# A decoder trunk on one core: the feed-forward output products in fp16 pairs, with scales found on the chip

## The chip, the core and the metric

The kernel runs on one NeuronCore of one Trainium2 chip. TensorE (PE in the profile) multiplies matrices from SBUF into PSUM banks of 128 rows by 512 columns, VectorE (DVE) and ScalarE (ACT) do the elementwise work, GpSimd (POOL) a little of it, and SyncE (SP) issues the transfers between device memory and SBUF. Each engine works through its own instructions in order and waits for the others by semaphores. The metric is the time of one execution on the device in microseconds (us), the median of several.

## What is computed

A trunk of two layers on 1024 tokens of width 1024, batch 1, in float32. Layer 0 mixes tokens with a gated linear recurrence (RG-LRU), layer 1 with stick-breaking attention; each is followed by a feed-forward part with 2816 hidden columns:

```python
def swiglu_ffn(x, w_in, w_out):
    gu = jnp.einsum("bsd,df->bsf", x, w_in)
    h = jax.nn.silu(gu[..., :D_FF]) * gu[..., D_FF:]
    return jnp.einsum("bsf,fd->bsd", h, w_out)

for layer in range(DEPTH):
    hn = rms_norm(h, mix_norm[layer])
    h = h + mixer(hn)
    h = h + swiglu_ffn(rms_norm(h, ffn_norm[layer]), ffn_w_in[layer], ffn_w_out[layer])
return rms_norm(h, final_norm)
```

## The kernel before

**Split operands.** To come near float32 on TensorE each operand is written as a high and a low part, and each block product takes three matmuls: high by high, high by low, low by high (`mm3`, lines 155 to 157). Two kinds of pairs occur. An *fp32r pair* takes two 4-byte tiles: ScalarE casts (CAST), VectorE subtracts (TENSOR_TENSOR). An *fp16 pair* takes half of the room, and its values are scaled by a power of two so that they fit: ScalarE multiplies by a one-column scale and rounds (ACTIVATE, line 834 for weights), VectorE computes value times scale minus high part (SCALAR_TENSOR_TENSOR, line 837). The power is found on the chip: squares are summed (ScalarE, line 827, with a running sum), added over the partitions by a small matmul (`over_partitions`, line 251), and VectorE makes the power out of the exponent bits in one-column operations (`power`, lines 244 to 248).

**Seven products.** Both halves of the feed-forward part use Winograd's form of Strassen's scheme: a product of 2 x 2 blocks with seven products, not eight. The weights come as two loads, `ra` and `rb`, of two half blocks each; VectorE forms sums of them (`s12`, `s2`, `s3`, `do_s4`), and these make four weight operands: a (products 0 and 1), b (2 and 4), c (3 and 5) and d (product 6). A step runs the products in the order 0, 1, 2, 3, 4, 6, 5. Products 0, 2, 4, 5 add up in one PSUM bank, 3 and 6 in another, 1 in a third; after each product its bank is copied by ScalarE or added by VectorE, and only then does the next product go on top.

**Input steps.** In each layer `mix_out_ffn_in` first finishes the mixer's output, then runs steps f = 0 to 21, one for each 128 hidden columns. Gate and up halves come out together; `gate` (lines 1126 to 1132) makes U = silu(gate) * up. Here all pairs are already fp16 (`Weights16`). The steps 4 to 19 go two by two (even and odd); there some inner products are shared by a second, smaller scheme (`inner_part`, tiles `it`, `is`, `i_ps`). `operands` stores the hidden blocks, two steps at a time, as p = 0 to 10, seven operands each, in device memory (`pd`).

**Output visits.** 13 visits u0 to u12 (12 in the last layer, whose u12 is done in `finish`) each take one pair of output columns d and a range of p:

```python
VISITS = (
    (0, 0, 2), (1, 0, 3), (2, 0, 4), (3, 0, 4), (0, 2, 5), (1, 3, 7), (2, 4, 8),
    (3, 4, 8), (0, 5, 9), (1, 7, 11), (2, 8, 11), (3, 8, 11), (0, 9, 11),
)
```

A visit of m = p1 - p0 blocks is 21 m matmuls of 512 columns. Here weights (`Weights`, lines 760 to 819) and hidden operands are fp32r pairs. `bring` loads an operand of p into SBUF as soon as the product that used its place has ended, and `split_op` (lines 1350, 1351) splits it two products later. The operands of p = 2 and 3 are split in advance, during the input steps 7 to 20 (`split_ahead`, lines 1330 to 1335), one per step, and go back to device memory as two tiles. `post_out` (lines 1413 to 1417) adds each product to the residual `h`.

**Order.** All engines but SP follow an order written out by hand: after product k of a step the code issues, one after another, the post-processing of that product, some preparation of this and the next step's weights, loads, `measure` (squares and powers for weights two steps ahead), `gate`, `operands`, `split_ahead` and the splits that are due. The first d of a layer (`w.d_hi`, `w.d_lo`) is made after the second of step 0's last products, behind the cast of step 1's a (`nw.a_hi`) and behind squares (`m2.square`).

## Time and profile before

| what | value |
|---|---|
| median of 3 runs | 2087.1 us (2086.4 to 2087.39) |
| the profiled execution | 2085.73 us, its span 2083.8 us |
| granted TensorE clock | 0.998 of full speed |
| step 0 of the input part, layer 0 and 1, starts near | 326 and 1452 us |
| visit u0, layer 0 and 1, starts at | 730.3 and 1854.8 us |

A row of a group reads: line, engine, operation, output <- inputs, shapes and types, count, then busy time in us and mean ns of one, then the idle time of the engine just before these instructions and who ended it. A row of the timeline reads: start, duration, engine, line, operation; in brackets how long the engine stood idle before it and who released it. A row of the windows reads: the stretch, its length, then for each engine its busy time and number of instructions, the granted clock and the share of the DMA engines. Matmuls overlap, so their durations (near 380 or 390 ns) say nothing of the rate; the time from one start to the next does.

### The profile page before, as it was taken

The page shows a single profiled execution, that of the slowest core. Times are in us where ns is not written, and L with a number is a line of the kernel's source. Part 1 is how long each engine was busy: PE and PEld are TensorE (multiplying, and loading weights), DVE is VectorE, ACT ScalarE, POOL GpSimd, SP SyncE. Part 2 cuts the span into 40 slices and gives each one's busy share as a digit, 9 for nine tenths or more (in the row PEclk, how much of TensorE's full clock was granted, in tenths as well). Part 3 has the DMA queues.
Part 4 walks back from the last instruction along what each step waited for, and adds up shares of the span by engine and source line. Part 5 has one row for each costly group of instructions (what it writes and reads, how often), then busy time and mean ns, then how long its engine had stood idle before and what let it go on. Part 6 is the DMA issues. An engine that isn't in the chain of part 4 may idle for free.

```text
span 2083.8 us, 28502 instructions
## 1 busy us (share of the span) xinstructions
PE 2059.5 (99%) x10052; PEld 1407.5 (68%) x10052; DVE 1816.4 (87%) x2805; ACT 1312.4 (63%) x2120; POOL 102.2 (5%) x114
## 2 busy tenths in 40 slices
PE   8999999999999999999999999999999999999998
PEld 7888885454545488888777777677445545458887
DVE  6887897989999889796999999977899999988786
ACT  6777446756656545466878788745766666554466
POOL 1000010000000000000011111202000000000002
PEclk9999999999999999999999999999999999999999
DMA  7231461544544646434888988962254544565442
GB/s 254 61 98 55 163 206 46 157 153 161 177 157 160 226 147 185 154 115 101 161 178 176 175 178 177 247 222 96 77 161 137 182 163 166 195 204 177 126 142 91
DMA packets 450607, 323.35 MB, mean 155 GB/s; under 512 B 166681, under 2 KB 362401, under 8 KB 450465
## 3 DMA queue, kind: packets, MB, share of 16 engines
q1 hardware_dynamic: 450304, 321.28, 53.8%
q8 instruction: 78, 1.28, 0.2%
q14 instruction: 65, 0.52, 0.1%
q10 hardware_dynamic: 160, 0.27, 0.0%
HBM read 193.01 MB, written 82.84 MB: 132 GB/s over the span
## 4 chain that ended last, share of the span: by engine, by line
PE 90%; DVE 6%; ACT 3%; DMA 1%; issue 1%; SPq 0%; DVEq 0%; ACTq 0%
PE p_ps L157 16%; PE p_ps L155 16%; PE p_ps L156 16%; PE qk_ps L155 4%; PE qk_ps L157 4%; PE qk_ps L156 4%; PE av_ps L2091 3%; PE a_ps L156 3%; PE a_ps L157 3%; PE a_ps L155 3%; PE ob_ps L155 3%; PE ob_ps L157 3%; PE ob_ps L156 3%; PE z_ps L1979 2%; PE z_ps L1980 2%; PE i_ps L155 1%
## 5 line engine op out<-in xcount | busy, mean ns | idle before, releaser
L157 PE MATMUL p_ps<-v,wb 128*128 128x512 f16 x352 | 133.6, 379 | 1.0 <-DVE wb L837 1.0
L156 PE MATMUL p_ps<-v,wb 128*128 128x512 f16 x352 | 133.4, 379 | 0.0
L155 PE MATMUL p_ps<-v,wb 128*128 128x512 f16 x352 | 133.4, 379 | 0.0
L157 PE MATMUL p_ps<-v,wc 128*128 128x512 f16 x352 | 133.4, 379 | 0.0
L156 PE MATMUL p_ps<-v,wc 128*128 128x512 f16 x352 | 133.4, 379 | 0.0
L155 PE MATMUL p_ps<-v,wc 128*128 128x512 f16 x352 | 133.3, 379 | 0.0
L834 ACT ACTIVATE wb<-sb,fac 128x1024 f16<-128x1024 f32 x44 | 50.5, 1147 | 103.6 <-DVE sb L766 103.6
L155 PE MATMUL qk_ps<-rh,whi 128*128 128x512 f32 x264 | 112.9, 428 | 0.0
L2039 ACT CAST wx<-w 128x512 f16<-128x512 f32 (+1 forms) x140 | 80.1, 572 | 41.4 <-DVE w L2024 21.1
L2017 ACT ACTIVATE w<-z_ps,rs 128x512 f32<-128x512 f32 (+2 forms) x168 | 96.8, 580 | 13.0 <-PE z_ps L1980 11.1
L156 PE MATMUL qk_ps<-rl,whi 128*128 128x512 f32 x264 | 103.5, 392 | 0.0
L157 PE MATMUL qk_ps<-rh,wlo 128*128 128x512 f32 x264 | 103.5, 392 | 0.0
L2024 DVE TENSOR_TENSOR_SCAN w<-w,unit 128x128 f32<-128x128 f32 (+1 forms) x112 | 93.4, 834 | 9.5 <-ACT w L2017 8.3
L155 PE MATMUL a_ps<-xh,whi 128*128 128x512 f32 x248 | 97.1, 391 | 0.0
L156 PE MATMUL a_ps<-xl,whi 128*128 128x512 f32 x248 | 96.6, 390 | 0.1
L157 PE MATMUL a_ps<-xh,wlo 128*128 128x512 f32 x248 | 96.6, 389 | 0.0
L1351 DVE TENSOR_TENSOR rl<-rl,rh 128x512 fp32r<-128x512 f32 x128 | 83.5, 686 | 4.9 <-ACT rh L1350 4.9
L232 POOL TENSOR_TENSOR acc<-acc,rbc 128x512 f32<-128x512 f32 x30 | 39.8, 1327 | 955.2 <-ACT rbc L231 703.8
L827 ACT ACTIVATE junk<-raw 128x1024 bf16<-128x1024 f32 x80 | 84.2, 1053 | 2.6 <-DMA raw<-in_ffn_w_in 2.5
L2040 DVE TENSOR_TENSOR wx<-w,wx 128x512 f16<-128x512 f32 (+1 forms) x140 | 85.5, 611 | 0.3 <-ACT wx L2039 0.2
L155 PE MATMUL p_ps<-v,wa 128*128 128x512 f16 x224 | 85.1, 380 | 0.0
L156 PE MATMUL p_ps<-v,wa 128*128 128x512 f16 x224 | 85.1, 380 | 0.0
(487 smaller groups left out, 6365.8 us busy)
## 6 DMA issues: line engine op xcount, KB each, us to landing
raw<-in_ffn_w_in SPq DMA_DIRECT2D x80, 512.0 KB, 4.1
rl<-pd SPq DMA_DIRECT2D x128, 256.0 KB, 3.3
pd<-U SPq DMA_DIRECT2D x90, 256.0 KB, 2.3
raw<-in_ffn_w_out SPq DMA_DIRECT2D x56, 256.0 KB, 3.3
raw<-in_attn_w_qkv SPq DMA_DIRECT2D x24, 512.0 KB, 4.2
raw<-in_lru_w_out SPq DMA_DIRECT2D x16, 512.0 KB, 3.5
h<-hd SPq DMA_DIRECT2D x32, 256.0 KB, 5.5
hd<-h SPq DMA_DIRECT2D x32, 256.0 KB, 2.5
```

What stands on the lines that cost most here:

```text
L155: nc.tensor.matmul(ps, lhsT=wh, rhs=mh, start=first, stop=False, **kw)
L156: nc.tensor.matmul(ps, lhsT=wh, rhs=ml, start=False, stop=False, **kw)
L157: nc.tensor.matmul(ps, lhsT=wl, rhs=mh, start=False, stop=last, **kw)
L827: nc.scalar.activation(v["junk"][:, 0 : t.shape[-1]], t, AF.Square, accum_out=next(at))
L834: nc.scalar.activation(hi, t, AF.Copy, scale=self.up)
L1351: V.tensor_sub(tl, f32(tl), f32(th))
L1979: nc.tensor.matmul(ps[:, 0 : c1 - c0], lhsT=lhsT, rhs=KK[q][hx][:, 0, c0:c1], start=True, stop=False)
L2017: nc.scalar.activation(F, ps[:, 0:n], AF.Sigmoid, scale=rs[:, j : j + 1])
L2024: nc.vector.tensor_tensor_scan(rev, rev, unit[:, NB - n :][:, ::-1], 0.0, op0=ALU.mult, op1=ALU.add)
L2039: nc.scalar.copy(wx[:, 0:m, 0], F)
L2040: nc.vector.tensor_sub(wx[:, 0:m, 1], F, wx[:, 0:m, 0])
L2091: nc.tensor.matmul(ps[:, c0:c1].rearrange("p (j c) -> p j c", c=P), lhsT=VV[q][:, hx, kb], rhs=t, start=first and i == 0, stop=last and i ...
```

## The change

1. Weights of the output visits are fp16 pairs too. The class `Weights` of fp32r pairs is gone, and `Weights16` becomes `Weights`, with a list of segments: columns k0 to k1 of each half and the scale for them. Each high or low part is made by one instruction per segment.
2. Hidden blocks fall in three classes: p = 0 to 3, 4 to 9, and 10. Each has its own power (`power_of`), found from sums of squares of U and of the output weights. A visit within one class scales all weights by one power; one that spans two (u4, u5, u9 to u12) has two segments whose powers make up for the difference. The result of a product is scaled back by `undo` when it is added to `h`.
3. For this ScalarE squares each U (`square_u`, 22 per layer) and each half row block of the output weights (`weigh_out`, 44 per layer, each with a load of 256 KB one step ahead), and at three points (`plan`) sums are added up and the scales made.
4. `split_ahead` runs in steps 10 to 20, two in each of 18 to 20, and stores one tile. An operand's raw values land in a tile of their own.
5. The weights' first sum is formed in place in `rb`, and c is made by one wide operation where `rb` is one tile. The target of the weights' squares, `junk`, gets a tile of its own.
6. The first d of a layer is made earlier: behind `v_last`, ahead of step 1's a.

```diff
         class Weights:
...
+            def cut(self, k0, k1, *ts):
+                for t in ts:
+                    if t.shape[-1] == NB:
+                        yield t[:, k0 * P : k1 * P]
+                    elif (k0, k1) == (0, HK):
+                        yield t
+                    else:
+                        yield t.rearrange("p (x c) -> p x c", x=2)[:, :, k0 * P : k1 * P]
 
             def high(self, hi, t):
-                nc.scalar.activation(hi, t, AF.Copy, scale=self.up)
+                for k0, k1, up in self.segs:
+                    h, r = self.cut(k0, k1, hi, t)
+                    nc.scalar.activation(h, r, AF.Copy, scale=up)
 
             def low(self, lo, t, hi):
-                V.scalar_tensor_tensor(lo, t, self.up, hi, op0=ALU.mult, op1=ALU.subtract)
+                for k0, k1, up in self.segs:
+                    l, r, h = self.cut(k0, k1, lo, t, hi)
+                    V.scalar_tensor_tensor(l, r, up, h, op0=ALU.mult, op1=ALU.subtract)
...
+            def s12(self):
+                self.sb = sp_.tile([P, S], F32, tag="sb", name="sb", bufs=1)
+                self.s4 = sp_.tile([P, NB], F32, tag="s4", name="s4", bufs=1)
+                V.tensor_sub(self.part(self.sb, 1), self.part(self.ra, 0), self.part(self.rb, 0))
+
+            def s2(self):
+                V.tensor_add(self.part(self.rb, 0), self.part(self.rb, 0), self.part(self.rb, 1))
...
             for j in range(HK):
                 v_last(h, v, j)
+            w.d_hi()
+            w.d_lo()
             nw.a_hi()
             nw.a_lo(2)
...
-                if k == 1:
-                    w.d_hi()
-                    w.d_lo()
...
-                return Weights(load, m)
+                groups = [int(p >= 4) + int(p >= 10) for p in range(p0, p1)]
+                g, m0 = groups[0], groups.count(groups[0])
+                cols_ = ((3,), (3,))[0] if m0 == m else (4, 5) if g == 0 else (6, 7)
+                segs = [(0, m0, gx[:, cols_[0] : cols_[0] + 1])]
+                if m0 < m:
+                    segs.append((m0, m, gx[:, cols_[1] : cols_[1] + 1]))
+                return Weights(load, m, segs)
...
+            def square_u(f):
+                nc.scalar.activation(GT[f % 2][:, NB:].bitcast(BF16), UT[f % 3], AF.Square, accum_out=psq(f))
+
+            def add_up(g):
+                p = part16[0]
+                with nc.allow_low_precision(reason="a bound alone"):
+                    if g == 0:
+                        V.tensor_reduce(p[:, 2:3], ymax[:, 0:8], axis=AX, op=ALU.add)
+                    elif g == 1:
+                        V.tensor_reduce(tmp[:, 0:1], ymax[:, 8:16], axis=AX, op=ALU.add)
+                        V.tensor_reduce(tmp[:, 1:2], wsq[0][:, 0:4], axis=AX, op=ALU.add)
+                        V.tensor_add(p[:, 2:3], tmp[:, 0:1], tmp[:, 1:2])
+                        V.tensor_reduce(p[:, 3:4], wosq[:, 0 : 2 * NF], axis=AX, op=ALU.add)
+                    else:
+                        V.tensor_add(p[:, 2:3], wsq[0][:, 4:5], wsq[0][:, 5:6])
...
+            def exponent(at, ps):
+                V.tensor_scalar(tmp[:, 0:1], ps, 1e-30, 1.0, op0=ALU.max, op1=ALU.mult)
+                V.tensor_single_scalar(H[:, at : at + 1], tmpi[:, 0:1], 24, op=ALU.logical_shift_right)
+
+            def both_of(a, at, i):
+                x, y = H[:, a : a + 1], H[:, a + 1 : a + 2]
+                t0, t1 = tmpi[:, 0:1], tmpi[:, 1:2]
+                V.tensor_max(t0, x, y)
+                V.tensor_add(t0, t0, H[:, 3:4])
+                for k, z in enumerate((x, y)):
+                    V.tensor_sub(t1, z, t0)
+                    V.tensor_scalar(t1, t1, -202.0, 203.0, op0=ALU.max, op1=ALU.add)
+                    V.tensor_scalar(G32[:, at + k : at + k + 1], t1, float(EXP), 0.0, op0=ALU.mult, op1=ALU.add)
+                inverse(t0, i)
+
+            def inverse(q, i):
+                field(H[:, 4 + i : 5 + i], q, 1, -25)
+                V.tensor_scalar_mul(sums[1][:, i : i + 1], rx_[:, 4 + i : 5 + i], -1.0)
+
+            def scales(g):
+                ps = pp.tile([P, NB], F32, tag="p", name="n_ps")
+                n = 2 if g == 1 else 1
+                over_partitions(ps[:, 0:n], part16[0][:, 2 : 2 + n])
+                exponent(g, ps[:, 0:1])
+                field(G32[:, g : g + 1], H[:, g : g + 1], -1, 203)
+                if g == 1:
+                    exponent(3, ps[:, 1:2])
+                    field(G32[:, 3:4], H[:, 3:4], -1, 203)
+                    for x in range(2):
+                        V.tensor_add(tmpi[:, 0:1], H[:, x : x + 1], H[:, 3:4])
+                        inverse(tmpi[:, 0:1], x)
+                    both_of(0, 4, 2)
+                elif g == 2:
+                    both_of(1, 6, 3)
...
+            def split_pair(hi, lo, raw, p):
+                nc.scalar.activation(hi, raw, AF.Copy, scale=power_of(p))
+                V.scalar_tensor_tensor(lo, raw, power_of(p), hi, op0=ALU.mult, op1=ALU.subtract)
+
+            def split_ahead(x, k):
+                if not 10 <= x <= 20:
                     return
...
+                now = (x - 10,) if x < 18 else (8 + 2 * (x - 18), 9 + 2 * (x - 18))
+                for y, at in enumerate(now):
+                    p, i = 2 + at // NPROD, ORDER[at % NPROD]
+                    if k == 0:
+                        nc.sync.dma_start(acc[at % 2], pd[p][i])
+                    elif k == 3 + 2 * y:
+                        split_pair(*pair16(rbc[at % 2]), acc[at % 2], p)
+                        nc.sync.dma_start(both[p, i].rearrange("p a b -> p (a b)"), rbc[at % 2].bitcast(F16))
...
                 if i in (0, 2, 3, 4):
                     src = spare(u)[i]
-                    nc.scalar.copy(src, ps)
-                if i in (3, 6):
-                    V.tensor_sub(t, t, src)
+                    nc.scalar.activation(src, ps, AF.Copy, scale=undo(u)[0])
+                    if i == 3:
+                        V.tensor_sub(t, t, src)
+                    else:
+                        V.tensor_add(t, src, t)
                 else:
-                    V.tensor_add(t, src, t)
+                    V.scalar_tensor_tensor(t, ps, undo(u)[i == 6], t, op0=ALU.mult, op1=ALU.add)
...
+            plan["f", 8, 4] = [lambda: add_up(0)]
+            plan["f", 8, 6] = [lambda: scales(0)]
+            plan["f", 20, 4] = [lambda: add_up(1)]
+            plan["f", 20, 6] = [lambda: scales(1)]
+            plan["v", 2, 4] = [lambda: add_up(2)]
+            plan["v", 2, 5] = [lambda: scales(2)]
+            spots = [(x, k) for x in range(2, 20) for k in ((1, 3, 6) if x % 2 else (0, 1))][: 2 * NF]
+
+            def weigh_out(i):
+                t = loose(v)
+                nc.sync.dma_start(t, ffn_w_out[layer][i // 2 * P : (i // 2 + 1) * P, i % 2 * NB : (i % 2 + 1) * NB])
+                x, k = spots[i]
+                plan.setdefault(("f", x, k), []).append(
+                    lambda: nc.scalar.activation(junk[:, 0:NB], t, AF.Square, accum_out=wosq[:, i : i + 1])
+                )
```

In the main loop the planned jobs of a product stand behind `measure` and ahead of `gate`; a U is squared one product after its last gate operation.

202 lines of the change are left out of this document (87 added, 115 removed).

## The prediction

> **What bounds the kernel now.** The page was read first, for the busy shares and for the chain that ended last; its time is that of this one execution.
>
> ```profile
> span 2083.8 us, 28502 instructions
> PE 2059.5 (99%) x10052; PEld 1407.5 (68%) x10052; DVE 1816.4 (87%) x2805; ACT 1312.4 (63%) x2120; POOL 102.2 (5%) x114
> PE 90%; DVE 6%; ACT 3%; DMA 1%; issue 1%; SPq 0%; DVEq 0%; ACTq 0%
> ```
>
> TensorE sets the end: nine tenths of the chain is its matmuls. So what counts is how fast a matmul follows the last one, and where VectorE (87% busy as a mean) gets too full to feed it. For that I asked for busy times by step: one of the input part, one pair of it, and six visits of the output part (u0, u4, u5, u6, u10, u11 of the first layer).
>
> ```profile
> core 0: us, PE busy (x) PEld busy (x) DVE busy (x) ACT busy (x) POOL busy (x), PEclk, DMA share, GB/s
> 389.21:407.36 18.15, 18.15 (x87) 8.22 (x86) 18.05 (x32) 10.26 (x18) 0.00 (x0) 1.00 0.47 155
> 550.47:568.80 18.33, 18.33 (x98) 9.32 (x97) 17.75 (x27) 12.18 (x20) 0.00 (x0) 1.00 0.60 199
> 568.80:586.33 17.53, 17.53 (x93) 8.82 (x92) 15.53 (x30) 9.99 (x17) 0.00 (x0) 1.00 0.45 137
> 730.30:740.95 10.65, 10.26 (x45) 7.76 (x43) 10.65 (x20) 7.27 (x15) 0.00 (x0) 1.00 0.72 228
> 793.31:807.78 14.47, 14.47 (x65) 11.74 (x64) 14.38 (x24) 9.43 (x18) 0.00 (x0) 1.00 0.68 213
> 807.78:826.82 19.04, 19.04 (x86) 15.77 (x85) 18.01 (x29) 10.92 (x18) 0.00 (x0) 1.00 0.53 161
> 826.82:845.86 19.04, 19.04 (x86) 15.77 (x85) 13.85 (x21) 7.68 (x13) 0.00 (x0) 1.00 0.19 56
> 902.98:917.26 14.28, 14.28 (x65) 11.83 (x64) 12.97 (x22) 8.40 (x16) 0.00 (x0) 1.00 0.32 106
> 917.26:931.81 14.55, 14.55 (x65) 11.73 (x64) 13.81 (x24) 9.20 (x17) 0.00 (x0) 1.00 0.40 127
> ```
>
> Two things are to be seen. A full step is 84 matmuls of 512 columns (7 products, 4 blocks, 3 each). In fp16 pairs it takes 18.15 us, 216.1 ns a matmul; in fp32r 19.04 us, 226.7 ns. And VectorE's load is uneven: full in u0, u4 and u5, idle for 5.2 us in u6. Idle time in u6 can't serve u4, since the work arrives at TensorE's pace.
>
> **The change part by part.** The groups by line give the matmuls that change form, and each operation beside its successor.
>
> ```profile
> L155 PE MATMUL p_ps<-rh,wah 128*128 128x512 f32 x172 | 67.3, 391 | 0.0
> L155 PE MATMUL p_ps<-rh,wd 128*128 128x512 f32 x86 | 34.0, 396 | 0.0
> L1351 DVE TENSOR_TENSOR rl<-rl,rh 128x512 fp32r<-128x512 f32 x128 | 83.5, 686 | 4.9 <-ACT rh L1350 4.9
> L649 DVE SCALAR_TENSOR_TENSOR v<-h,gx,v 128x512 f16<-128x512 f32 x16 | 11.3, 746 | 0.6 <-ACT v L648 0.6
> L1350 ACT CAST rh<-rl 128x512 fp32r<-128x512 f32 x128 | 73.1, 621 | 0.0
> L648 ACT ACTIVATE v<-h,gx 128x512 f16<-128x512 f32 x16 | 10.6, 707 | 0.0
> ```
>
> *Matmuls.* The a, b and c weights have three such groups each, d three of 86: 9 x 172 + 3 x 86 = 1806 matmuls, each 10.6 ns closer to the next: 19.1 us, and some 0.4 us for the 512- and 256-column ones of `finish`. **Gain 19.5 us**, if nothing else is late. The rule that speaks against it is in the Trainium skill, TensorE: Matmul & The Clock Gate, Back-to-back issue gap: 2.5 ns over the columns at 2.4 GHz, about 216 ns at 512 columns, with no term for the type. By it fp32r would run at 216 ns already and this term would be 0; the rows above have 226.7 against 216.1, and I go by them.
>
> *d of the first weights, earlier.*
>
> ```profile
> PE ob L155 <- ACT wd L834: 4.9, 2, 2.5
> ...
> 344.24 0.39 PE L155 MATMUL ob<-v,wd 128*128 128x512 f16 x1 [2.46 <-ACT wd L834]
> ...
> 336.95 2.56 ACT L681 ACTIVATE v<-h,gx 128x512 f16<-128x512 f32 x4
> ...
> 343.47 0.72 ACT L834 ACTIVATE wd<-s,fac 128x512 f16<-128x512 f32 x1
> ...
> 337.70 2.74 DVE L682 SCALAR_TENSOR_TENSOR v<-h,gx,v 128x512 f16<-128x512 f32 x4
> ...
> 356.53 1.28 DVE L232 TENSOR_TENSOR acc<-acc,rbc 128x512 f32<-128x512 f32 x2
> ...
> 340.00:350.00 10.00, 7.36 (x27) 2.64 (x25) 9.28 (x15) 6.39 (x12) 0.00 (x0) 0.83 0.00 1
> ...
> 1470.00:1480.00 10.00, 9.53 (x45) 4.21 (x46) 9.49 (x15) 5.36 (x9) 0.00 (x0) 1.00 0.11 30
> ```
>
> Its cast now stands right behind L681, so at 339.5 instead of 343.5, and its low part behind L682, from 340.4 to 341.1; TensorE asks at 341.6. What it is moved ahead of, the cast and low part of step 1's a, ends 0.6 us later, near 342.6, and is asked for at 344.3. That frees 2.6 us, 0.3 us of a second wait for the low part, and in layer 0 the half clock that followed (0.83 over 10 us is 3.4 us at half rate: 1.7 us; layer 1 kept 1.00). Next late are the sums of squares before `stats_mm`: VectorE ended them at 357.8 and reaches them 2.1 us sooner (the wd between is gone, and most of a wait for ScalarE), at 355.7; TensorE, 48 matmuls into step 1, would come at 354.8. So 0.9 us are handed back. Layer 0 gains 3.7, layer 1 2.0: **gain 5.7 us** (bounds 3 and 7.5).
>
> *VectorE in the visits.* A subtraction becomes SCALAR_TENSOR_TENSOR: 746 - 686 = 60 ns more. It hits each split, the low parts of a, b, d and three additions to h per visit. In the six visits that mix classes (u4, u5, u9 to u12) each of the weights' operations is cut in two. What a cut costs is read from one wide operation and two narrow ones, start to start:
>
> ```profile
> 703.92 0.15 DVE L244 TENSOR_SCALAR sums<-n_ps 128x1 f32<-128x1 f32 x1
> 704.11 0.15 DVE L246 TENSOR_SCALAR sums<-sums 128x1 int32<-128x1 int32 x1
> ...
> 708.12 0.69 DVE L1117 TENSOR_TENSOR U<-U 128x512 f32<-128x512 f32 x1 [0.61 <-ACT U L1116]
> ...
> 714.66 1.28 DVE L837 SCALAR_TENSOR_TENSOR wb<-sb,fac,wb 128x1024 f16<-128x1024 f32 x1
> 715.86 0.75 DVE L837 SCALAR_TENSOR_TENSOR wc<-s,fac,wc 128x512 f16<-128x512 f32 x1
> 716.52 0.75 DVE L837 SCALAR_TENSOR_TENSOR wc<-raw,fac,wc 128x512 f16<-128x512 f32 x1
> ...
> 721.69 0.75 DVE L837 SCALAR_TENSOR_TENSOR wd<-s,fac,wd 128x512 f16<-128x512 f32 x1 [1.94 <-ACT wd L834]
> ...
> 788.81 0.69 DVE L1417 TENSOR_TENSOR g<-held,g 128x512 f32<-128x512 f32 x1 [0.35 <-ACT held L1413]
> ...
> 806.78 1.22 DVE L778 TENSOR_TENSOR wal<-raw,wah 128x1024 fp32r<-128x1024 f32 x1
> ...
> 818.92 0.69 DVE L1351 TENSOR_TENSOR rl<-rl,rh 128x512 fp32r<-128x512 f32 x1 [0.17 <-ACT rh L1350]
> ```
>
> 1.20 us against 2 x 0.66: a cut costs 0.12 us. u4 and u5: between the waits at 788.81 and 818.92 VectorE never stands still. To the end of a's low part at 808.0 it has 13 splits (0.8 us), a, b, c, d of mixed weights with the next a (0.8) and three STTs on h (0.2): 1.8 us later, while TensorE, 24 + 63 matmuls on, asks 0.9 us sooner. That low part had 0.3 us in hand (808.24 was u5's third matmul), and u5, mixed too, adds 0.5: TensorE loses about **2.9 us a layer**. ScalarE, 90 ns longer per split, delays the copy out of the bank that product 6 needs by a like amount, beside it.
>
> u9 to u12: in layer 0 u10 and u11 leave VectorE 1.3 and 0.7 us, TensorE's time shrinks by 0.7 each, and VectorE's grows by 0.9 each (u12 too): **3.0 us** of the gain are not had. In layer 1, with less to do per visit, the last visits before `finish` lose **1.2 us**.
>
> *Scales and sums at step 20.* Behind U L1117 (708.12, which waits for TensorE's product 4) VectorE gets four reductions (0.6 us), a second `split_ahead` (0.7) and the 22 one-column operations of `scales(1)`: from 0.07 us where independent to 0.19 where chained (703.92 to 704.11), I take 3.3 us. Queued behind them is b's low part for step 21, which ended at 715.9; TensorE asks for it near 718.1. 4.6 us on 2.3 us of slack: **2.3 us a layer**. The scale matmul comes at TensorE's own step end, before VectorE is there; `scales(0)` has three such operations at step 8, which loses its split, and the 13 of `scales(2)` (2 us) lie ahead of 3 us of slack in u3: nothing, or 0.3 us.
>
> *u0.* VectorE runs without a gap from the wd at 721.69 above to the low part of u0's d, for which TensorE waits:
>
> ```profile
> 738.67 0.50 PE L157 MATMUL p_ps<-rh,wd 128*128 128x512 f32 x1 [0.39 <-DVE wd L809]
> ```
>
> 14 splits, three low parts and one STT on h add 1.1 us, the square of U ahead of two splits on ScalarE some 0.4; with the 0.5 us that TensorE would have gained, **2.0 us a layer**.
>
> *Squares in the input steps.* ScalarE squares U (22) and the output weights (44) in each layer:
>
> ```profile
> L827 ACT ACTIVATE junk<-raw 128x1024 bf16<-128x1024 f32 x80 | 84.2, 1053 | 2.6 <-DMA raw<-in_ffn_w_in 2.5
> 571.43 0.16 DVE L925 TENSOR_REDUCE part<-sums 128x1 bf16<-128x4 f32 x1 [1.37 <-ACT junk L827]
> ```
>
> 1.24 us for U and 0.8 for each half row of weights make 3.3 us a step, on ScalarE, idle for 7.5 of 17.5 us in odd steps and 6.2 of 18.3 in even ones. Uncovered it would be paid whole. The even steps already hold VectorE to 97%, with 0.16 us of TensorE waiting for b each time a split ran before (six a layer). Two of these go, since `split_ahead` starts three steps later; four grow by 0.2 us: **1.0 us lost** in all (bounds -1 and +12). The 44 loads a layer of 256 KB stand on SP's queue a step ahead of use; DMA is at half load there. Against them stand 14 stores and 14 loads saved.
>
> At nothing: two narrow c operations become one wide (0.12 us less on an engine that isn't late there), fewer weight tiles, sums in place behind squares that were read a step before.
>
> Sum: gains 19.5 + 5.7 = 25.2; losses 2 x 2.9 + 4.2 + 2 x 2.3 + 2 x 2.0 + 1.0 = 19.6. That is 5.6 us less: 2083.8 becomes a span of 2078.2. The profiled execution took 2085.7 us, 1.9 around its span; the median of the runs shown is 2087.1, 1.4 above it. Forecast **2081.5 us**.
>
> **The rivals.** *VectorE's lead covers it.* Low parts are made up to a step ahead, so the visits might swallow 1.5 us each; for it speaks that u10 ran with waits of VectorE, against it that u0 and u4 stall now. A quarter of the losses left: 25.2 - 4.9, about 2067.
>
> *ScalarE becomes the bound in the input steps* (slower). In an odd step VectorE waits 1.37 us for a square at 571.43, and b's low part stands behind that wait. If the new squares delay this one by over 1.4 us plus the 1 us b has in hand, TensorE waits in each pair from step 4 on: 1.2 us x 8 pairs x 2 layers = 19 us, 2081.5 + 19 = 2100; at half that 2091. Against it: ScalarE's waits for TensorE in these steps are in all longer than the squares.
>
> *The clock drops.* 2.5 us of idling cost half clock in layer 0 and none at 1470 in layer 1. New stalls of 2 to 3 us at step 21, u0 and u4, two layers, could bring four drops of 1.7 us: 2088. By the Trainium skill (TensorE: Matmul & The Clock Gate, The HAM clock gate) it needs an idle window of about 3.4 us, which would give 0 here; the gap of 2.5 us above did it.
>
> *The matmuls don't get closer,* if something other than the type holds them 226.7 ns apart (two operands of one tile, say): 19.5 us less gain, 2101.
>
> **How the numbers follow.** Forecast 0.48, lead covers 0.21, ScalarE 0.14, clock 0.13, no closer matmuls 0.04. About 0.2%, 4.2 us, is what a measurement of this kernel can tell from no change: faster is under 2082.9. Of the forecast's own range (2074 to 2089, half or one and a half of the losses) 0.6 lies below: 0.29 + 0.21, with 0.02 of the clock's, is 0.52 faster. Slower: 0.14 and 0.04 less 0.02 that end under 2091.3, with 0.02 of the forecast's, 0.18. The same: 0.30. The range leaves out the lower half of the second case and the upper half of the third: 2066 to 2093.
>
> **What would show it.** Matmuls of the output part 216 ns apart and no wait for wd at the start of either layer; a wait of TensorE for wb near step 21 of 2 us or more, u4 near 16 us and u6 at 18.1; even input steps within 0.3 us of 18.3. Wrong would be: u0, u4 and u11 without stalls (then my VectorE sums have the wrong start), or input steps over 19 us.

## The result, and the profile after

| kernel | median, us | ratio to the kernel before [95% interval] |
|---|---|---|
| before, beside it | 2086.75 (4 runs) | |
| changed | 2097.58 (4 runs, 2095.29 to 2099.97) | 1.0053 [1.0035, 1.0070] |

The change makes the kernel slower by half a per cent, 10.8 us; 5.6 us less had been forecast. Its four runs line up with the TensorE clock that each was granted: 2095.29 us at 1.000, 2096.64 at 0.999, 2098.52 at 0.998, 2099.97 at 0.996. The profiled execution took 2096.64 us. The page of the changed kernel, with its span, the busy times and the chain that ended last:

```profile
span 2094.5 us, 28835 instructions
...
PE 2042.5 (98%) x10058; PEld 1240.3 (59%) x10058; DVE 1853.6 (88%) x2878; ACT 1437.9 (69%) x2369; POOL 104.4 (5%) x114
...
PE 71%; DVE 19%; ACT 6%; issue 3%; DMA 1%; SPq 0%; DVEq 0%; ACTq 0%
```

TensorE is busy for 17 us less than before, and still the span is 10.7 us longer. VectorE has 19% of the chain, where it had 6%: TensorE now waits. For whom is in the waits of PE in the changed kernel (total in us, times, longest):

```profile
PE p_ps L157 <- DVE wb L775: 10.3, 11, 2.3
PE p_ps L155 <- ACT G L1458: 4.9, 5, 2.1
PE p_ps L155 <- ACT held L1458: 4.4, 3, 1.9
PE n_ps L251 <- DVE part L1304: 3.1, 2, 1.6
```

Four kinds: for the low part of b (`wb`), for two kinds of copies of a product's bank (`post_out`, L1458), and for the sum that goes into the small matmul of `scales` (L1304 in `add_up`). Before, the largest of them was the wait for wd, 4.9 us in all, and it is gone. The windows of the changed kernel, layer 0: the last products of step 0, step 3, step 21, u0, u2, u4, u5, u6 and u9.

```profile
core 0: us, PE busy (x) PEld busy (x) DVE busy (x) ACT busy (x) POOL busy (x), PEclk, DMA share, GB/s
335.82:342.30 6.48, 6.48 (x32) 2.94 (x31) 6.32 (x11) 6.38 (x12) 0.00 (x0) 1.00 0.01 3
384.40:403.93 19.53, 18.49 (x87) 8.16 (x86) 19.10 (x33) 13.28 (x23) 0.00 (x0) 1.00 0.60 193
710.68:731.34 20.66, 18.40 (x87) 8.06 (x85) 19.08 (x45) 12.18 (x20) 0.00 (x0) 1.00 0.55 172
731.34:743.13 11.79, 9.89 (x44) 3.89 (x43) 11.79 (x20) 8.91 (x15) 0.00 (x0) 1.00 0.95 305
756.74:776.62 19.88, 18.31 (x87) 8.25 (x86) 19.07 (x30) 9.92 (x12) 0.00 (x0) 1.00 0.33 112
794.75:810.54 15.79, 13.92 (x65) 6.15 (x64) 15.79 (x28) 12.62 (x22) 0.00 (x0) 1.00 0.86 264
810.54:829.59 19.05, 18.50 (x86) 7.98 (x85) 18.88 (x30) 11.35 (x19) 0.00 (x0) 1.00 0.46 141
829.59:847.72 18.13, 18.13 (x86) 8.20 (x85) 15.39 (x22) 9.71 (x13) 0.00 (x0) 1.00 0.20 59
883.98:904.21 20.23, 18.29 (x86) 8.22 (x85) 19.84 (x33) 15.59 (x28) 0.00 (x0) 1.00 0.20 66
```

The same stages before, as far as they were not shown yet (the last products of step 0, step 21, u2 and u9):

```profile
337.61:348.32 10.71, 8.07 (x32) 3.06 (x31) 9.99 (x17) 8.78 (x16) 0.00 (x0) 0.89 0.01 2
...
712.35:730.30 17.95, 17.95 (x85) 8.11 (x84) 15.35 (x24) 11.04 (x20) 0.00 (x0) 1.00 0.59 201
755.23:774.27 19.04, 19.04 (x86) 15.77 (x85) 17.11 (x24) 8.00 (x11) 0.00 (x0) 1.00 0.32 104
883.94:902.98 19.04, 19.04 (x86) 15.77 (x85) 17.81 (x29) 13.19 (x24) 0.00 (x0) 1.00 0.29 97
```

u6 shows the gain pure: 18.13 us for 84 matmuls, 215.8 ns each, where it was 19.04. u5 has the same matmuls and 0.92 us of waiting, u2 1.75, u9 2.1. Read every visit so: its length against 4.53 us for each block of p, that is 18.13 us for four, 13.60 for three and 9.06 for two.

Stage by stage, from the first matmul with a's weights of one step to that of the next, before and after (us; layer 1 in brackets where it differs by over 0.1):

| stage | before | after |
|---|---|---|
| step 0's last products and step 1 | 32.79 (31.10) | 29.01 |
| steps 2, 3, 4 | 18.81, 18.16, 18.16 | 19.56, 19.53, 18.46 |
| steps 5 to 11 | 17.53 and 18.16 to 18.33 | 17.53 and 18.16 to 18.19 |
| each of steps 12, 14, 16, 18 | 18.33 | 18.59 |
| step 20 | 18.44 (18.58) | 19.20 (19.09) |
| step 21 | 17.94 | 20.66 (22.35) |
| u0 / u1 | 10.65 / 14.28 | 11.79 / 13.61 |
| u2 / u3 | 19.04 / 19.04 | 19.88 / 18.13 |
| u4 / u5 | 14.47 / 19.04 | 15.79 / 19.05 |
| u6, u7, u8, each | 19.04 | 18.13 |
| u9 / u10 / u11 | 19.04 / 14.28 / 14.55 (19.04 / 14.28 / 15.35) | 20.23 / 14.62 / 15.69 (20.37 / 14.25 / 16.81) |

This table, not the span, carries what follows: where nothing was changed, nearly all stages of the kernels below agree within 0.03 us, while the kernel's start moves by up to 3.4 us between profiles (here 1.8 us in favour of the changed kernel) and step 20 by 0.9 us (19.04 and 18.15 in the two layers of b_d_early, which changes nothing in it).

How a wait comes about is best seen in u9. Three engines in the timeline of the changed kernel (start, duration, engine, line, operation; the idle time before it and who ended it):

```profile
889.38 3.16 ACT L1365 ACTIVATE v<-raw,gx 128x512 f16<-128x512 f32 x5
...
894.87 0.72 ACT L235 ACTIVATE xg<-g,vc 128x512 fp32r<-128x512 f32 x1 [1.76 <-DVE g L1464]
...
898.44 1.24 ACT L1458 ACTIVATE held<-p_ps,rx 128x512 f32<-128x512 f32 x2
...
890.12 1.40 DVE L775 SCALAR_TENSOR_TENSOR wc<-raw,gx,wc 128x768 f16<-128x768 f32 x2
891.45 2.73 DVE L1366 SCALAR_TENSOR_TENSOR v<-raw,gx,v 128x512 f16<-128x512 f32 x4
894.10 0.74 DVE L1464 SCALAR_TENSOR_TENSOR g<-p_ps,rx,g 128x512 f32<-128x512 f32 x1
...
899.16 0.38 PE L155 MATMUL p_ps<-v,wd 128*128 128x512 f16 x1 [1.94 <-ACT held L1458]
```

VectorE makes c's low part (cut in two) and four splits, and only then adds product 1 to h (894.10). ScalarE's next instruction needs that h, and stands idle for 1.76 us; behind it in its order are a square, d, a, a split, and the copy of the bank in which product 6 is to add up (898.44). TensorE gets it 1.94 us late. ScalarE is busy for 15.6 of 20.2 us here: it isn't full, it is held up in the wrong order.

### The profile page after: what moved, and what is told of

Its sections match the earlier page's. It is cut to its first block, busy times and chain, and to the rows that moved or that the text cites. A ratio compares the mean times of both kernels' runs of the same rounds, so it can differ in the third digit from the quotient of the medians.

```text
span 2094.5 us, 28835 instructions
## 1 busy us (share of the span) xinstructions
PE 2042.5 (98%) x10058; PEld 1240.3 (59%) x10058; DVE 1853.6 (88%) x2878; ACT 1437.9 (69%) x2369; POOL 104.4 (5%) x114
## 3 DMA queue, kind: packets, MB, share of 16 engines
q8 instruction: 78, 1.28, 0.3%
## 4 chain that ended last, share of the span: by engine, by line
PE 71%; DVE 19%; ACT 6%; issue 3%; DMA 1%; SPq 0%; DVEq 0%; ACTq 0%
PE p_ps L157 10%; PE p_ps L155 10%; PE p_ps L156 10%; PE qk_ps L155 4%; PE qk_ps L157 4%; PE qk_ps L156 4%; PE av_ps L2163 3%; PE a_ps L156 3%; PE a_ps L157 3%; PE a_ps L155 3%; PE ob_ps L155 3%; PE ob_ps L156 3%; PE ob_ps L157 3%; DVE v L1366 2%; DVE wa L775 2%
## 5 line engine op out<-in xcount | busy, mean ns | idle before, releaser
L157 PE MATMUL p_ps<-v,wb 128*128 128x512 f16 x524 | 199.5, 381 | 10.5 <-DVE wb L775 10.3
L155 PE MATMUL p_ps<-v,wb 128*128 128x512 f16 x524 | 199.0, 380 | 5.5 <-ACT G L1079 2.4
L157 PE MATMUL p_ps<-v,wc 128*128 128x512 f16 x524 | 198.6, 379 | 2.4 <-DVE wc L775 2.4
L156 PE MATMUL p_ps<-v,wb 128*128 128x512 f16 x524 | 199.3, 380 | 0.0
L155 PE MATMUL p_ps<-v,wc 128*128 128x512 f16 x524 | 198.6, 379 | 0.0
L156 PE MATMUL p_ps<-v,wc 128*128 128x512 f16 x524 | 198.6, 379 | 0.0
L157 PE MATMUL p_ps<-v,wa 128*128 128x512 f16 x396 | 150.1, 379 | 0.0
L156 PE MATMUL p_ps<-v,wa 128*128 128x512 f16 x396 | 150.1, 379 | 0.0
L155 PE MATMUL p_ps<-v,wa 128*128 128x512 f16 x396 | 150.0, 379 | 0.0
L155 PE MATMUL p_ps<-v,wd 128*128 128x512 f16 x254 | 96.2, 379 | 11.1 <-ACT G L1458 4.9
L157 PEld LDWEIGHTS <-wb 128*128 128x128 f16 x524 | 51.3, 98 | 80.7 <-DVE wb L775 22.6
L1366 DVE SCALAR_TENSOR_TENSOR v<-raw,gx,v 128x512 f16<-128x512 f32 x128 | 91.1, 745 | 7.8 <-ACT v L1365 7.6
L157 PE MATMUL p_ps<-v,wd 128*128 128x512 f16 x254 | 96.3, 379 | 1.5 <-DVE wd L775 1.5
```

What stands on the lines that cost most here:

```text
L155: nc.tensor.matmul(ps, lhsT=wh, rhs=mh, start=first, stop=False, **kw)
L156: nc.tensor.matmul(ps, lhsT=wh, rhs=ml, start=False, stop=False, **kw)
L157: nc.tensor.matmul(ps, lhsT=wl, rhs=mh, start=False, stop=last, **kw)
L1366: V.scalar_tensor_tensor(lo, raw, power_of(p), hi, op0=ALU.mult, op1=ALU.subtract)
```

## The experiments

All kernels are the changed one with the edit shown, unless said otherwise. The ratio is to the kernel before, run beside each of them; its medians lay between 2085.92 and 2086.79 us, so differences between medians in the text carry up to 0.9 us of that. The stages carry less.

| kernel | median, us (runs) | ratio [95% interval] |
|---|---|---|
| b_d_early | 2079.36 (5) | 0.9968 [0.9956, 0.9981] |
| a_scales1 | 2095.14 (5) | 1.0039 [1.0025, 1.0052] |
| a_scales2 | 2094.74 (5) | 1.0043 [1.0031, 1.0056] |
| a_late | 2089.60 (11) | 1.0016 [1.0007, 1.0025] |
| a_spots | 2103.40 (5) | 1.0082 [1.0069, 1.0095] |
| a_noweigh | 2094.23 (5) | 1.0035 [1.0022, 1.0047] |
| a_nosq | 2091.76 (7) | 1.0027 [1.0015, 1.0038] |
| a_pool | 2249.83 (4) | 1.0785 [1.0770, 1.0800] |
| a_oneclass | 2091.73 (6) | 1.0028 [1.0017, 1.0040] |
| a_cap3 | 2098.91 (5) | 1.0058 [1.0046, 1.0071] |
| a_late_pooladd | 2110.97 (4) | 1.0119 [1.0105, 1.0133] |
| a_two | 2084.48 (11) | 0.9989 [0.9980, 0.9998] |
| a_two_due | 2084.83 (11) | 0.9990 [0.9981, 0.9999] |
| a_two_spots | 2083.60 (11) | 0.9983 [0.9974, 0.9992] |
| a_best | 2082.15 (9) | 0.9979 [0.9970, 0.9989] |
| a_best2 | 2082.24 (11) | 0.9979 [0.9970, 0.9988] |
| b_d_again | 2079.02 (5) | 0.9964 [0.9950, 0.9978] |

### The earlier d alone: b_d_early

In the kernel before:

```diff
                 v_last(h, v, j)
+            w.d_hi()
+            w.d_lo()
             nw.a_hi()
...
-                if k == 1:
-                    w.d_hi()
-                    w.d_lo()
```

> The kernel before with only the first d of each layer made behind v_last; nothing of the fp16 pairs. Stage by stage the changed kernel was 3.8 us (layer 0) and 2.1 us (layer 1) shorter up to the end of step 1. If the move alone did this, the time is 5.9 us below the kernel before (2080.9 us of 2086.8), with no wait of TensorE for wd. Rival: the room came from the other edits of these steps (a tile of its own for junk, sums in place), and the move alone gives under 3 us.

6.6 us less, and its windows have the changed kernel's two stages to 0.03 us (step 0's last products, step 1):

```profile
337.46:343.96 6.50, 6.50 (x32) 2.92 (x31) 6.38 (x11) 6.44 (x13) 0.00 (x0) 1.00 0.01 3
343.96:366.48 22.52, 22.19 (x119) 11.64 (x117) 19.31 (x38) 17.12 (x29) 0.00 (x0) 1.00 0.10 28
```

So this part of the change is worth 5.9 us by itself, and all the rest of it costs about 17.

### The scales: a_scales1, a_scales2, a_late

```diff
-            plan["f", 20, 4] = [lambda: add_up(1)]
-            plan["f", 20, 6] = [lambda: scales(1)]
+            plan["f", 20, 6] = [lambda: add_up(1)]
+            plan["f", 21, 1] = [lambda: scales(1)]
```

> The changed kernel with add_up(1) two products later and scales(1) behind product 1 of step 21, so behind wb and wc. Theory of single waits: the 2.4 us wait of TensorE for wb in step 21 goes in both layers, and with it the 3.4 us of half clock in layer 1 (1.7 us): 2 x 2.4 + 1.7 = 6.5 us less, 2091.1 us. Rival, the backlog: VectorE is busy 92% in step 21 and 100% in u0, so the 2.4 us come back as longer waits in step 21 and u0, and the time falls by 1.7 to 2.5 us only, 2095 to 2096.

Both were right in part. Step 21 fell to 18.45 us in both layers, with no half clock; u0 grew by 1.05 us, since TensorE now waits there 1.13 us for a copy (L1458). And a wait of 2.25 us in u9 of layer 1 that had not cost the clock now did, 1.7 us. In all 2.4 us less.

```diff
-            plan["v", 2, 4] = [lambda: add_up(2)]
-            plan["v", 2, 5] = [lambda: scales(2)]
+            plan["v", 3, 0] = [lambda: add_up(2)]
+            plan["v", 3, 1] = [lambda: scales(2)]
```

> The changed kernel with add_up(2) and scales(2) in u3 (behind products 0 and 1), not u2. Theory of single waits: TensorE's own 1.73 us wait for the sum, ahead of the matmul of scales(2), goes in both layers: 3.5 us less, 2094.1 us. Rival, the backlog: VectorE, 96% busy in u2, then makes TensorE wait by as much in u2 or u4: no change within 1 us.

u2 fell by 1.75 us to 18.13, u3 rose by 0.80: the small matmul came one product after its sum was issued, and again stood still for VectorE. 2.8 us less.

a_late divides the chain where VectorE has idle time. For u0 only the sum of the output weights and the first class's scale are needed; these are the new `add_up(3)` and `scales(3)`:

```diff
+            plan["f", 19, 6] = [lambda: add_up(3)]
+            plan["f", 20, 1] = [lambda: scales(3)]
+            plan["v", 0, 6] = [lambda: add_up(1)]
+            plan["v", 1, 1] = [lambda: scales(1)]
+            plan["v", 5, 4] = [lambda: add_up(2)]
+            plan["v", 6, 0] = [lambda: scales(2)]
```

> The changed kernel with the scales made in four places, not three: the sum and power of the output weights and the scale of the first class in step 20 (behind product 1), those of the second class in u1 and of the third in u6. With all of scales(1) behind product 1 of step 21 the step lost its 2.4 us wait but u0 grew by 1.05 us; with scales(2) in u3 u2 lost 1.75 us and u3 grew by 0.8. Theory: a chain of one-column operations costs only where VectorE has no idle time; step 20, u1 (14% idle) and u6 have it. Step 21 falls to 18.4, u0 stays at 11.8, u2 falls to 18.13, u3 stays at 18.13: 2 x (2.2 + 1.75) + 1.7 for the half clock = 9.6 us less, 2088. Rival, the backlog: u0 grows by 1 us all the same and u1 or u2 by another 1: 2 x 2 less, 2092.

8.0 us less, with no half clock in its profile (1.7 us of the difference between the two profiles). The windows of step 21 and u2:

```profile
709.72:728.01 18.29, 18.29 (x86) 8.14 (x85) 16.28 (x23) 12.23 (x21) 0.00 (x0) 1.00 0.64 205
753.68:771.81 18.13, 18.13 (x86) 8.22 (x85) 17.89 (x24) 9.60 (x12) 0.00 (x0) 1.00 0.33 109
```

TensorE shows no idle time in either, u0 stayed at 11.79 us, and u1 grew by 0.27. The same operations cost 8 us in the one place and next to nothing in the other: these were single waits, not a backlog.

### The squares: a_spots, a_noweigh, a_nosq, a_pool

```diff
-            spots = [(x, k) for x in range(2, 20) for k in ((1, 3, 6) if x % 2 else (0, 1))][: 2 * NF]
+            spots = [(x, k) for x in range(5, 20) for k in ((1, 3, 5, 6) if x % 2 else (0, 1))][: 2 * NF]
```

> The changed kernel with the squares of the output weights in steps 5 to 19 only (four in an odd step), none in steps 2 to 4. Theory: these squares on ScalarE made steps 2 to 4 longer by 2.4 us a layer (57.55 against 55.13 us); without them the steps go back and the odd steps, with 40% of ScalarE idle, take them: 4.8 us less, 2092.8 us. Rival: the squares of U did it, or the sums in place: no change within 1 us. Second rival: odd steps with four squares grow by 0.3 us each, and it is paid back.

Steps 2 to 4 fell by 1.5 us a layer, and the odd steps stayed at 17.53, but the even steps 6 to 18 grew by 0.6 us each: 5.8 us more. The timeline of ScalarE around the start of step 12 shows why, with TensorE's wait as the last row:

```profile
550.32 0.61 ACT L1514 ACTIVATE junk<-raw 128x512 bf16<-128x512 f32 x1
...
551.39 0.63 ACT L1514 ACTIVATE junk<-raw 128x512 bf16<-128x512 f32 x1
...
552.02 1.14 ACT L770 ACTIVATE wc<-raw,fac 128x1024 f16<-128x1024 f32 x1
553.06 0.56 ACT L1079 COPY G<-p_ps 128x512 f32<-128x512 f32 x1
...
553.67 0.38 PE L155 MATMUL p_ps<-v,wb 128*128 128x512 f16 x1 [0.87 <-ACT G L1079]
```

Two squares issued at the end of the odd step stand ahead of c and of the copy of the next step's first product, and product 2 waits for that bank. The odd step gets the square, the even step pays for it.

a_noweigh:

```diff
-            for i, (x, k) in enumerate(spots):
-                plan.setdefault(("f", x - 1, k), []).append(lambda i=i: weigh_out(i))
+            V.memset(wosq, 0.18)
```

> The changed kernel without the 44 loads and squares of the output weights in each layer (their sum is a constant). Theory, ScalarE: with the squares in steps 5 to 19 steps 2 to 4 were 1.5 us a layer shorter and the even steps 0.6 us longer each, so the squares delay ScalarE's copies. Without them steps 2 to 4 are at 56.0 us or below (57.55 in the changed kernel), and the even steps 12 to 18 lose their 0.43 us wait (18.59 to 18.16): 2 x (1.5 + 1.7) = 6.4 us less, 2091. Rival: the squares of U and the later split_ahead make the even steps longer: they stay at 18.59, 3 us less, 2094.5.

3.4 us less. Steps 2 to 4 took 56.03 us as expected; the even steps 12 to 18 stayed near 18.52 as the rival had it: there the copy isn't late any more, but b's low part is, by the same amount. a_nosq has this too, and:

```diff
-                    for f in squares_of:
-                        square_u(f)
-                    del squares_of[:]
...
+            plan["f", 2, 3] = [lambda: V.memset(ymax, 300.0), lambda: V.memset(wsq[0][:, 0:6], 300.0)]
```

> The changed kernel without any of the new squares: neither those of the output weights (44 a layer, with their loads) nor those of U (22 a layer); constants stand for their sums. Without the weights' squares alone steps 2 to 4 took 56.03 us (57.55 in the changed kernel, 55.13 before) and the even steps 12 to 18 still 18.52 (18.33 before). Theory: the squares of U are the rest, so steps 2 to 4 go back to 55.1 to 55.4, the even steps to 18.33 or below, and u2 to 18.13 (add_up(2) waits for the last of them): 2 x (0.8 + 0.8 + 1.7) = 6.6 us under the kernel without the weights' squares, 2087.6. Rival: what is left in steps 2 to 4 comes from the sums in place in another order; then only u2 and the even steps change, 2089.2 or more.

2.5 us less again. The windows of step 3, first without the weights' squares, then without any:

```profile
386.79:405.73 18.94, 18.39 (x87) 8.13 (x86) 18.80 (x33) 11.96 (x20) 0.00 (x0) 1.00 0.53 172
```

```profile
384.81:403.02 18.21, 18.21 (x87) 8.15 (x86) 18.07 (x32) 10.19 (x18) 0.00 (x0) 1.00 0.45 155
```

With ScalarE at 13.28, 11.96 and 10.19 us of work the step takes 19.53, 18.94 and 18.21. Steps 2 to 4 end at 55.30 (55.13 before): the squares of the weights are 1.5 us of their loss a layer, those of U 0.7. u0 gained 0.35 us. But the even steps 12 to 18 stayed at 18.51, so neither kind of square holds them there; what does wasn't tested. And u2 stayed at 19.88: `add_up(2)` doesn't wait for a square, it stands behind `gate`, `operands` and a's low part in VectorE's order.

a_pool, where the sum takes one of the twelve places that the loads had:

```diff
-                    lambda: nc.scalar.activation(junk[:, 0:NB], t, AF.Square, accum_out=wosq[:, i : i + 1])
+                    nc.gpsimd.tensor_mul(t, t, t)
+                    if i:
+                        nc.gpsimd.tensor_add(wsum[0], wsum[0], t)
```

> The changed kernel with the squares of the output weights on GpSimd (one product and one addition of 128 x 512, 1.3 us each as its rows for L232 have them), and one reduction on VectorE at the end; the loads stay. Theory: ScalarE's time alone is what counts, so it comes out as without these squares: 3.4 us less than the changed kernel, 2094.2, steps 2 to 4 at 56.0. Rival: GpSimd and VectorE hinder each other, VectorE's operations beside it grow, and the steps with two or three squares get longer by 0.5 us or more: 2100 or above.

152 us more: in layer 0 steps 2 to 4 took 20 to 25 us and steps 5 to 7 31 to 43. From step 8 on, when GpSimd had finished, they were as in a_noweigh. What VectorE's operations took between 430 and 553 us, in a_pool and in a_noweigh:

```profile
L1104 DVE SCALAR_TENSOR_TENSOR U<-U,fac,G 128x1024 f32<-128x1024 f32 x4 | 7.9, 1978 | 0.0
...
L1089 DVE TENSOR_TENSOR U<-U 128x512 f32<-128x512 f32 x4 | 5.7, 1424 | 0.5 <-ACT U L1088 0.5
...
L1102 DVE TENSOR_TENSOR G<-ob,G 128x1024 f32<-128x1024 f32 x3 | 3.6, 1212 | 0.0
```

```profile
L1103 DVE SCALAR_TENSOR_TENSOR U<-U,fac,G 128x1024 f32<-128x1024 f32 x7 | 9.0, 1279 | 0.0
...
L1101 DVE TENSOR_TENSOR G<-ob,G 128x1024 f32<-128x1024 f32 x7 | 8.5, 1218 | 0.0
...
L1088 DVE TENSOR_TENSOR U<-U 128x512 f32<-128x512 f32 x7 | 4.8, 691 | 3.3 <-ACT U L1087 3.0
```

The squares also didn't come two or three a step: GpSimd and its loads ran ahead, and all 44 of layer 0 were done by the end of step 7, 29 of them in steps 5 to 7. So the run is a test of a GpSimd that is busy without a pause, not of squares spread over 18 steps. The rival, hindrance, is shown for VectorE under that load: 1.98 us for 1.28, 1.42 for 0.69. It isn't all: ScalarE also waited once for 20.9 us for input weights, whose loads stand in SP's queue behind the loads for GpSimd (three of them held it for 7.1 us). How the 152 us divide is left open.

### Cuts, order and load in the visits: a_oneclass, a_cap3, a_late_pooladd

a_oneclass, with the first class's power in `undo` and `power_of` as well:

```diff
-                if m0 < m:
-                    segs.append((m0, m, gx[:, cols_[1] : cols_[1] + 1]))
-                return Weights(load, m, segs)
+                return Weights(load, m, [(0, m, gx[:, 3:4])])
```

> The changed kernel with one power for all hidden blocks, that of p = 0 to 3, so that no weight operation is cut in two; the small operations for the other scales stay. Theory of the prediction: 0.12 us a cut, 0.8 us of the 2.9 us of u4 and u5, and about 0.5 us in each of u9 to u12 on VectorE, as much on ScalarE. The waits in u4, u5 and u9 to u12 shrink by some 0.6 us each and the time by 2 x 2.5 = 5 us. Rival: the cuts stand beside waits that the runs of splits set (six in a row ahead of the copy that product 6 of u4 waits for); then u4's 1.77 us and u9's 2.1 us stay, and the time falls by under 1.5 us.

5.9 us less. u9 fell from 20.23 to 19.29 us, u10 of layer 0 from 14.62 to 13.86, u11 from 15.69 to 15.30; u4 by only 0.55, of which u5 gave back 0.15. So the cuts cost 0.4 us a layer in u4 and u5, half of what had been counted, and 2 to 3 us a layer in u9 to u12.

```diff
-                        while tasks and tasks[0][0] <= now:
-                            split_op(*tasks.pop(0)[1:])
+                        for _ in range(3):
+                            if tasks and tasks[0][0] <= now:
+                                split_op(*tasks.pop(0)[1:])
```

> The changed kernel with at most three splits issued behind one product of a visit (up to six in the changed kernel); those over it wait for the next product. Theory: in u4 six splits in a row (3.8 us) stand on ScalarE ahead of the copy of the bank that product 6 needs, and in u9 five; with three the 1.77 and 2.1 us waits fall by a half or more, and no other wait grows: 2 x 1.8 = 3.6 us less, 2094. Rival: it is the sum of the work in u4 and u5 that is too much for ScalarE and VectorE, not its order; then u5 grows by what u4 loses: no change within 1 us.

A miss for u4 (15.79 still: its six splits stand behind products 0 and 1, three each, and ScalarE has nothing to copy between them); u9 fell by 0.66 us in both layers, and u10 of layer 0 gave 0.2 of it back. The median didn't fall; in the profiled run both waits in step 21 brought the half clock, where one did in the changed kernel, and that is 1.7 us against the 1.3.

a_late_pooladd, in `post_out` of a_late:

```diff
                     if i == 3:
-                        V.tensor_sub(t, t, src)
+                        nc.gpsimd.tensor_sub(t, t, src)
                     else:
-                        V.tensor_add(t, src, t)
+                        nc.gpsimd.tensor_add(t, src, t)
```

> The kernel with the scales in four places (2089.6 us), and in every visit the four additions to h of a copied product (0.69 us each on VectorE) on GpSimd. Theory: in u0, u4, u5 and u9 to u12 VectorE has too much work, and 2.8 us less of it a visit take away most of the waits that are left there (about 7.5 us a layer against the rate of 215.8 ns a matmul): 2 x 4 us or more, 2081 or below. Rival: ScalarE's order sets these waits; they stay, 2088 to 2090. Second rival: GpSimd and VectorE hinder each other, so that VectorE's other operations grow by more than they are relieved: 2092 or above.

21 us more than a_late: the second rival. The group of VectorE's splits, first without, then with GpSimd's additions beside them:

```profile
L1364 DVE SCALAR_TENSOR_TENSOR v<-raw,gx,v 128x512 f16<-128x512 f32 x128 | 91.2, 746 | 7.8 <-ACT v L1363 7.6
```

```profile
L1364 DVE SCALAR_TENSOR_TENSOR v<-raw,gx,v 128x512 f16<-128x512 f32 x128 | 103.1, 837 | 6.5 <-ACT v L1363 6.3
```

The additions also take 1.4 to 1.6 us each on GpSimd and were 0.7, and what uses h comes later by that. The profile also has three drops to half clock, together 5.1 us, where a_late's has none. How much is which wasn't told apart.

### Together: a_two, a_two_due, a_two_spots, a_best, a_best2, b_d_again

a_two is a_late with two classes, so that no boundary lies at p = 10:

```diff
-                groups = [int(p >= 4) + int(p >= 10) for p in range(p0, p1)]
+                groups = [int(p >= 4) for p in range(p0, p1)]
...
+            plan["v", 2, 5] = [lambda: add_up(1)]
+            plan["v", 3, 0] = [lambda: scales(1)]
```

> The kernel with the scales in four places (2089.6 us), now with two classes, p = 0 to 3 and 4 to 10, the second found at the end of u2: only u4 and u5 mix classes, and the third scale's chain is gone. With one class u9 to u12 were shorter by 2.9 us in layer 0 and about 2 in layer 1. Theory: these waits shrink because the weights' operations there are not cut, so the same comes here: 4.9 us less, 2084.7, with u9 at 19.3 to 19.4 us, u10 of layer 0 at 13.9. Rival: the chain behind u3's first product makes u4's a late, and u3 or u4 gives back 1 us or more a layer, 2087 or above.

2084.48 us, 5.1 less than a_late, and u9 in the window:

```profile
881.64:900.93 19.29, 18.29 (x86) 8.19 (x85) 19.14 (x29) 14.66 (x23) 0.00 (x0) 1.00 0.22 69
```

u3 and u4 gave nothing back (18.16 and 15.79). By the stages the cuts are about 4.5 us of the loss in u9 to u12, in a kernel that still finds its scales.

a_two_due:

```diff
-                            tasks.append((L * (x + 1) + k + 2 + y, p + 4, i))
+                            tasks.append((L * (x + 1) + k + 1 + y, p + 4, i))
```

> The kernel with two classes, and each split of a hidden operand due one product after its load instead of two. Theory, the order: u4 has too many splits and u3 has room, so two splits go from u4 to u3 and the 1.77 us wait in u4 falls by 1 us or more, and the one in u9 likewise: 2 x 1.5 us less than with two classes. Rival, the loads: 2.6 us are too short for a load of 256 KB, ScalarE waits for it in its order, and the copies behind it come later: 2 us or more above it.

No change: u4 0.16 us shorter, u5 0.16 longer. Nor did the rival come. In u4 and u5 it is the sum of the work, not its order.

a_two_spots:

```diff
-            spots = [(x, k) for x in range(2, 20) for k in ((1, 3, 6) if x % 2 else (0, 1))][: 2 * NF]
+            spots = [(x, k) for x in range(2, 20) for k in ({2: (0,), 3: (2, 3), 4: (0, 1), 19: (0, 1, 2, 3)}.get(x) or ((1, 2, 3) if x % 2 else (0, 1)))][: 2 * NF]
```

> The kernel with two classes, and the squares of the output weights behind products 1, 2 and 3 of the odd steps (and 0 and 1 of the even ones, with one, two and two only in steps 2, 3 and 4). In the kernel with four squares in odd steps, two of them behind products 5 and 6, the even steps grew by 0.6 us each. Theory: a square hurts where ScalarE's next copy is due, the last one of an odd step; with none there the even steps 12 to 18 lose up to 0.4 us each and steps 3 and 4 some 0.3: 3 us less than with two classes. Rival: three squares in a row delay gate in the odd step; the odd steps leave 17.53 and it is paid back.

0.9 us less, inside the intervals, where 3 were expected. Steps 2 and 4 fell by 0.6 and 0.25 us, step 3 stayed at 19.53, and the even steps 12 to 18 at 18.55: with the copy in time b is late, as in a_noweigh.

a_best has the edits of a_two_spots and a_cap3.

> The kernel with two classes, these places for the squares, and at most three splits behind a product of a visit (u9 fell by 0.66 us with that in both layers). If the parts add up: 2084.7 - 3 - 1.1 = 2080.6 us, faster than the kernel before by 0.3%, and no better than the kernel before with the early d alone (2079.4). If the waits only move: 2084 to 2086.

2082.15 us: 2.3 less than a_two, not 4.1. u9 fell to 18.63 us (18.77 in layer 1), u10 of layer 0 rose by 0.45.

a_best2 leaves step 3 out of these places and puts four squares in steps 5 and 7.

> The kernel with two classes, at most three splits a product, and the squares of the output weights as in the one before, but with none in step 3 (four in steps 5 and 7). Step 3 still took 19.53 us there; without these squares it took 18.94. Theory of place: 2 x 0.6 us less than 2082.15, so 2081.0, and steps 5 and 7 stay at 17.53. Rival: steps 5 and 7 hand it back, no change.

A miss: step 3 took 19.53 us without any square of weights in it. Only the kernels without them in steps 2 and 4 too had it at 18.94. What sets it is open.

b_d_again is b_d_early once more.

> The kernel before with the early d alone, a second time, beside the best version with fp16 pairs on one chip. From the earlier run 2079.4 us: if the waits that are left in u0, u4, u5 and u9 to u12 (about 7 us a layer with fp16 pairs) eat what the closer matmuls give, the two stand within 2 us of each other.

2079.02 us against 2082.24: 3 us apart in favour of the kernel before with the early d alone. Both beat the kernel before, and nothing tried with fp16 pairs beat that one move.

## Why the prediction was wrong

The prediction added 25.2 us of gains and 19.6 of losses. The gains were right. The losses, each the change of the stage plus, in the visits, the 10.6 ns a matmul that it should have gained, were twice as large, 38.2 us (both layers, us):

| term | predicted | measured | shown by |
|---|---|---|---|
| closer matmuls | 19.5 | 18.13 for 19.04 us a full visit without waits, as said | u3, u6 to u8 |
| earlier d | 5.7 | 5.9 | b_d_early |
| u4, u5 | -5.8 | -5.8 | |
| u0 | -4.0 | -3.2 | |
| steps 20 and 21 | -4.6 | -8.4, 1.7 of it half clock | a_late |
| u9 to u12 | -4.2 | -11 | a_two, a_cap3 in part |
| squares in input steps | -1.0 | -6.3 | a_nosq: 4.5 of them |
| scales(2) in u2 | 0 or -0.3 | -3.5 | a_scales2, a_late |

**The step that failed** is that of u9 to u12. It took VectorE's idle time in u10 and u11 (1.3 and 0.7 us) and set it against VectorE's growth; u9 came out free, and ScalarE, called late "by a like amount, beside it" in u4, was not counted here at all. u9 then lost 2.1 us, more than any of the others. What the runs showed in its place is the order across two engines in the timeline above: VectorE's run of splits holds an addition to h, that holds ScalarE, and ScalarE holds the bank. About 4.5 us of the 11 are the cuts (a_two), 1.3 the run of splits in u9 (a_cap3). The rest, about 5 us, is argued, not shown: the 60 and 90 ns on each operation, at a TensorE that comes sooner. Not all of it is that order: in u11 of layer 0 TensorE waited for VectorE alone, as the prediction had it, 0.8 us for c's low part and 0.5 for b's. This step is 7 us of the 18.6 by which the losses were too small; the three that follow are the rest.

**u2.** "Nothing, or 0.3 us" priced 13 one-column operations behind slack in u3. It left out that the matmul of `scales(2)` is TensorE's own instruction: whatever VectorE has queued ahead of its operand is TensorE's wait. The sum was issued one product ahead of it, and VectorE, at work without a gap from 765.61 us, came to it at 773.93; TensorE stood idle for 1.57 us.

**Squares.** 1.0 us was chosen between bounds of -1 and +12; what was priced were TensorE's six short waits for b in the even steps, and the squares' time on ScalarE was thought covered by its idle time. The even steps came out near that, 1.4 us. In steps 2 to 4, which had no price, ScalarE's order isn't covered: 2.2 us a layer, 4.5 in all (a_nosq).

**Steps 20 and 21.** The wait is the predicted 2.3 us (2.42), in both layers. On top came 1.7 us of half clock in layer 1, which the prediction had as a rival, and step 20, which varies by 0.9 us by itself. The price of the chain (3.3 us for 22 operations) was right: VectorE was at it from 713.05 to 716.47 in the changed kernel.

**u4, u5 and u0** were right in size. In u0 TensorE waits for low parts, d's among them, as predicted. In u4 the wait that ended last was not the one that the sum was worked out from, a's low part on VectorE, but the one named "beside it". ScalarE has no idle time from 797.08 us on, and these stand ahead of product 6:

```profile
798.67 3.77 ACT L1365 ACTIVATE v<-raw,gx 128x512 f16<-128x512 f32 x6
...
806.06 0.67 ACT L1458 ACTIVATE held<-p_ps,rx 128x512 f32<-128x512 f32 x1
...
806.78 0.38 PE L155 MATMUL p_ps<-v,wd 128*128 128x512 f16 x1 [1.61 <-ACT held L1458]
```

VectorE was full too, and a's low part about as late as foretold (it ended at 811.69 us, 16.9 us into the visit; 808.0 + 1.8 is 16.5 us into it); TensorE, held up in u4, no longer had to wait for it. So the size of 2.9 us fits VectorE and ScalarE alike, and the agreement is partly luck. (The 808.24 us from which the prediction took 0.3 us of slack is 808.36 in the timeline of the kernel before.) In u4 and u5 the cuts are 0.4, not 0.8 us a layer; something else makes up for it, and it isn't the order of the splits.

**The rivals.** VectorE's lead covered little: u0, u4, u5 and u9 to u11 all wait. ScalarE did hold up input steps, but chiefly three of them, not each pair from step 4 on, and by the copies of banks and by b's low part (0.3 and 0.8 us in step 3), not by the wait at a square; that its 2091 to 2100 us hold the measured time is luck, since these steps are 6 us of the 19 that it had. The clock dropped once in the profile where four drops were priced. Matmuls did get closer, with two operands in one tile.

## What to carry to other kernels

Where engines keep a written order, a new instruction costs what is queued behind it and needed first: look for the next copy out of a bank on ScalarE, and for matmuls whose small operand VectorE makes, before adding up busy time. Put such work where the engine has idle time of its own, and pull a long chain apart by when each result is needed: that alone gave back 8 of the 17 us here. And take a change apart before judging it: the moved d gave the whole net gain, and the rest, mended as far as it went, still cost 3 us.
